# Stick-breaking attention over the prompt: weights formed on VectorE, or the running product applied to differences of values

## The chip, the cores and the metric

One NeuronCore of one Trainium2 chip runs the whole step in one launch. The metric is device time in microseconds (us) of one execution; three executions were timed, and the median is what counts.

## The reference, cut to what matters

One layer of a hybrid encoder trunk: a prompt of 1024 tokens and a sample of 32 tokens with 128 cached positions, model width 1024. A combined projection of the normed input feeds three mixers (an S5 state-space mixer, a gMLP spatial gate, and stick-breaking attention with 8 heads of 64) and three sigmoid gates of 1024 columns each. The gated sum is projected, added, and followed by a SwiGLU. What the change touches is this:

```python
z = einsum("bhtd,bhsd->bhts", q, k) * 64 ** -0.5
causal = k_pos < q_pos
log_1m = where(causal, log_sigmoid(-z), 0)
between = cumsum(log_1m, reverse=True) - log_1m
wts = where(causal, exp(log_sigmoid(z) + between), 0)
o = einsum("bhts,bhsd->bhtd", wts, v)
```

With C(s) the product of sigmoid(-z) over all keys from s to the last, the weight of key s is sigmoid(z(s)) * C(s+1), which is also C(s+1) - C(s).

## The kernel before, in words

All projections are fp32-accurate: every operand is split into a high and a low part (type fp32r), and each product is three matmuls, `mm3` (L142 to L145). A unit of weights, 128 x 1024, is loaded to `raw` (L112), its high part is copied by ScalarE (L116) and its low part subtracted by GpSimd (L117, `split_weights`). The buffers of the weights are a ring of four, two for `raw`.

The program goes through these stages, and on each engine instructions run in the order in which a scheduler has put them at compile time:

- Norm of the input; attention values `v_dense` (L234): a value block is copied from PSUM (L251), written out, then split into high and low halves side by side (L259 on ScalarE, L260 on VectorE) and stored to the DRAM scratch `v_d`. Beside it VectorE computes the tables of the S5 mixer (L396 to L605; L42 to L45 is a complex product, L553 the first transposes on TensorE that need its result, L135 the add that frees a PSUM tile of the sample's values).
- q and k of four pairs of heads (`qk_dense`), the spatial gate, the S5 mixer.
- The prompt's attention (`attention`, L731): 32 units of (pair of heads, block of 256 queries, head). `load_head` (L734) fetches the keys and the split values. `stage_a` (L749) forms z, masks it with a product of `identb` and `maskb`, takes sigmoid(-z) into `om` (L776) and sigmoid(z) into `sg` (L777) on ScalarE, and on VectorE the reversed running product (L779, a scan) and the weights (L780):

```python
v.tensor_tensor_scan(rev, rev, rev, 1.0, op0=OP.mult, op1=OP.bypass)
v.tensor_mul(sg[:, 0:n], sg[:, 0:n], om[:, 1:n + 1])
```

  `stage_b` (L784) transposes the weights by TensorE (L797, tile `p_t`), splits them (L805 ScalarE, L806 VectorE; `wth`, `wtl`, on the diagonal `wd`) and applies them to the values (L813, L814, tile `p_av`); the output of each unit is joined and split again (L826 to L829) and stored to `y_d`. Stage A of a unit is written beside stage B of the unit before.
- Between these steps `fill` (L939) takes steps of other work off a list: the remaining q and k, and `gate_ahead` (L921), which computes gate tiles ahead of their turn, three branches of 24 matmuls each (tile `p_d`, L143 to L145), stored to `sig_d`. `AHEAD = (7, 0)` (L87) says how many of the 8 gate tiles of each half of the tokens are made ahead. These instructions have a lower priority (`LATER`), so that the scheduler alone decides where they go.
- The sample's attention (L872), in front of the last unit. What is left of the list follows.
- The gated merge of half 0 (`gates`, L1005), in which tile 7 is computed and tiles 0 to 6 are read back from `sig_d` (`sgg`), the output projection (L1057), then the merge of half 1 with all its gate tiles computed there, the second norm, and the feed-forward in groups of 256 columns (L1100, L1141).

Of the kernel before, what the change touches and what calls it, by code (L numbers as in the profile page):

```python
# [29 lines left out]
EPS = 1e-6  # L30
# [18 lines left out]
def trunk_kernel(ctx: ExitStack, tc: tile.TileContext,  # L49
# [19 lines left out]
    ring = ctx.enter_context(pool("ring", 4))  # L69
# [9 lines left out]
    q_d = [dram.tile([2, 2, 64, T], F32, name=f"q_d{i}") for i in range(4)]  # L79
    k_d = [dram.tile([2, 2, 64, T], F32, name=f"k_d{i}") for i in range(4)]  # L80
    v_d = [dram.tile([TP, 256], F32, name=f"v_d{i}") for i in range(4)]
# [22 lines left out]
    def split_weights(src, hi=None, lo=None):  # L104
        wh = hi if hi is not None else ring.tile([128, 1024], F32R, name="wh")
        wl = lo if lo is not None else ring.tile([128, 1024], F32R, name="wl")
        raw = ring.tile([128, 1024], F32, name="raw", bufs=2)
# [19 lines left out]
    def tm_sample(ps, xt2, us):  # L127
        # rows 0..31: high parts of the sample, rows 32..63: low parts
# [28 lines left out]
    def rstd_of(wk, ss, rows, more=EPS):  # L157
        # 1 / sqrt(ss + more + EPS), from a first guess in the exponent bits
# [39 lines left out]
    # =====================================================================================  # L198
    # Input projection, mixers
    # =====================================================================================  # L200
    xn = [(half_tile(hx, f"xnh{h}", "hx"), half_tile(hx, f"xnl{h}", "hx")) for h in range(2)]

    with ExitStack() as ph1:
        ps1 = ph1.enter_context(pool("ps1", 2, PSUM))
        qk = ph1.enter_context(pool("qk", 1))
# [6 lines left out]
        # sample attention operands kept on chip  # L212
# [21 lines left out]
        def v_dense(wk):  # L234
            us = v_units
            for b, hc in [(b, hc) for b in range(6) for hc in range(2)] + [(b, hc) for hc in range(2) for b in (8, 6, 7)]:
# [17 lines left out]
                vc = wk.tile([128, 4, 128], F32R, name="vc", bufs=2)  # L254
                v4 = v32.rearrange("p (h d) -> p h d", d=64)
                for e in range(2):
                    o = 64 * e
                    hi = vc[:, e::2, o:o + 64]
# [8 lines left out]
        def qk_dense(wk, hp):  # L267
# [20 lines left out]
            # k first: it goes out beside the products of q  # L288
# [107 lines left out]
        def s5_setup(pl, keep):  # L396
# [175 lines left out]
            # the two groups of a pair side by side: rows (g2, c)  # L572
# [50 lines left out]
        def s5_main(pl, S):  # L623
# [70 lines left out]
            # GLU  # L694
# [36 lines left out]
        def attention(at, qk_tasks):  # L731
            cnt = [0]

            def load_head(hp, h2):  # L734
                kt = at.tile([128, TP], F32R, name="kst", bufs=2)
# [6 lines left out]
            ck = sample_past(at)  # L742
            # the first quarter of these stays zero: keys after all queries
            diags = [[at.tile([128, 512], F32R, name=f"wd{i}{e}") for e in range(2)] for i in range(2)]
            for d in diags:
                for a in d:
                    g.tensor_scalar(a[:, 0:128], ident, 0.0, None, op0=OP.mult)

            def stage_a(hp, tp, h2):  # L749
# [3 lines left out]
                q2 = at.tile([128, 2, 256], F32R, name="q2", bufs=3)  # L753
# [4 lines left out]
                for tt in range(2):  # L758
# [23 lines left out]
                    yield ws, 2 * n / 2400.0 + 0.06  # L782

            def stage_b(hp, tp, h2, ws):  # L784
                vt = heads[hp, h2][1]
                av = ps_tile("av")[:, 0:256]
# [36 lines left out]
                a, b = slice(64 * h2, 64 * h2 + 64), slice(64 - 64 * h2, 128 - 64 * h2)  # L823
                yo = at.tile([128, 2, 256], F32R, name="yo", bufs=1)
                ty = yo[:, 1].bitcast(F32)
                s.activation(ty[a], av[b], AF.Copy)  # L826
                v.tensor_add(ty[a], av[a], ty[a])
                s.activation(yo[a, 0], ty[a], AF.Copy)
                v.tensor_sub(yo[a, 1], ty[a], yo[a, 0].bitcast(F32))  # L829
                o = 256 * (tp % 2)  # L830
                sp.dma_start(y_d[4 + hp][tp // 2].rearrange("l p t -> p l t")[a, :, o:o + 256], yo[a].bitcast(F32))
# [11 lines left out]
            for i, u in enumerate(units):  # L843
# [19 lines left out]
                if i == 30:  # L863
                    sample_attention(at, ck)

# [1 line left out]
        def sample_past(wk):  # L867
            ck = wk.tile([128, 8, 64], F32, name="ck")
# [3 lines left out]
        def sample_attention(wk, ck):  # L872
# [4 lines left out]
            cv = wk.tile([128, 1024], F32, name="cv", tag="kst", bufs=2)  # L877
# [5 lines left out]
            for gr in range(2):  # L883
# [4 lines left out]
                # rows (head, t): keys 128.. are visible before t  # L888
                sg = wk.tile([128, 1024], F32, name="sgs", tag="sg", bufs=4)[:, 0:160]
                om = wk.tile([128, 1025], F32, name="oms", tag="om", bufs=3)[:, 0:161]  # L890
# [22 lines left out]
            yo = wk.tile([128, 2, 256], F32R, name="yos", tag="yo", bufs=1)[:, :, 0:128]  # L913
# [304 lines left out]
```

## Time and profile before

| what | value |
|---|---|
| median of three timed executions | 1812.64 us (1804.2, 1812.64, 1814.32) |
| span of the profiled execution, first to last instruction | 1798.5 us |
| outside the span, against the median | 14.1 us |
| mean granted clock of TensorE, share of full speed | 0.981 |
| TensorE matmul busy | 1692.1 us, 94% of the span |
| VectorE, ScalarE, GpSimd busy | 42%, 31%, 30% |

The profiled execution's own time is not listed beside its span; the timed executions lie 5.7 to 15.8 us above it. The shares are means over stages that differ much: the table of stages in the rows below shows where TensorE is not busy. A granted clock of 1.00 is 2.4 GHz; 0.50 would be 1.2 GHz.

### The profile page before, as it was taken

What the parts mean: (1) busy time and instruction counts of PE and PEld (TensorE: products, weight loads), DVE (VectorE), ACT (ScalarE), POOL (GpSimd) and SP (SyncE); (2) the same over time, 40 slices, a digit from 0 to 9 for tenths busy, and PEclk for the clock granted to TensorE, in tenths of its full rate; (3) what the DMA queues carried; (4) which work ended last, traced back from release to release, by engine and by line L of the source; (5) the groups of instructions that cost most, each with busy time, mean ns of one, the idle gap of its engine ahead of it and who ended that gap; (6) DMA issues with size and microseconds to landing.
All of it is one profiled execution on the core that took longest, in us unless ns stands there. A gap on an engine that the chain in (4) does not pass through costs nothing.

```text
span 1798.5 us, 26081 instructions
## 1 busy us (share of the span) xinstructions
PE 1692.1 (94%) x10421; PEld 1489.7 (83%) x10421; DVE 750.3 (42%) x1498; ACT 564.0 (31%) x1066; POOL 542.7 (30%) x397
## 2 busy tenths in 40 slices
PE   6889998997887899999999899999999999999997
PEld 6879887776565677999999798889889889888885
DVE  7964525259999546112235602121131230221215
ACT  5323232356676422223223422112112111111124
POOL 2211212331112133444443233334233223233344
PEclk9999999999999899999999999999999999999998
DMA  6553252574444187423431111111111111111112
GB/s 206 152 131 92 97 133 73 155 230 144 129 129 113 45 269 250 136 84 93 129 95 60 59 47 48 47 48 48 47 37 50 43 36 48 48 47 48 47 34 87
DMA packets 224617, 171.51 MB, mean 95 GB/s; under 512 B 34608, under 2 KB 202576, under 8 KB 224496
## 3 DMA queue, kind: packets, MB, share of 16 engines
q1 hardware_dynamic: 224496, 169.84, 32.0%
q8 instruction: 82, 1.34, 0.3%
q14 instruction: 39, 0.32, 0.1%
HBM read 131.25 MB, written 37.96 MB: 94 GB/s over the span
## 4 chain that ended last, share of the span: by engine, by line
PE 59%; DVE 4%; ACT 2%; issue 1%; DMA 1%; SPq 0%; POOL 0%; POOLq 0%; DVEq 0%; ACTq 0%
PE p L144 19%; PE p L145 19%; PE p L143 19%; PE p L1160 1%; DVE rs_m L168 1%; DMA y<-y_d 1%; DVE rs_m L169 1%; DVE xb L180 0%; PE ptn L185 0%; DMA raw<-in_w_out_dram 0%; PE p_t L797 0%; DVE sg L780 0%; DVE h L1170 0%; DVE yo L829 0%; ACT junk L1173 0%
## 5 line engine op out<-in xcount | busy, mean ns | idle before, releaser
L117 POOL TENSOR_TENSOR wl<-raw,wh 128x1024 fp32r<-128x1024 f32 x164 | 403.4, 2465 | 713.6 <-ACT wh L116 630.0
L144 PE MATMUL p<-x,wh 128*128 128x272 f32 (+1 forms) x1056 | 342.3, 324 | 0.0
L143 PE MATMUL p<-x,wh 128*128 128x272 f32 (+1 forms) x1056 | 341.5, 323 | 0.0
L145 PE MATMUL p<-x,wl 128*128 128x272 f32 (+1 forms) x1056 | 341.4, 323 | 0.0
L116 ACT ACTIVATE wh<-raw 128x1024 fp32r<-128x1024 f32 x164 | 172.7, 1059 | 475.6 <-PE p L145 190.5
L1116 DVE TENSOR_TENSOR sl<-p,sl 128x272 f32<-128x272 f32 (+1 forms) x66 | 34.6, 525 | 463.8 <-PE p L145 463.8
L143 PEld LDWEIGHTS p<-x,wh 128*128 128x128 f32 x1056 | 198.8, 188 | 16.0
L144 PEld LDWEIGHTS p<-x,wh 128*128 128x128 f32 x1056 | 198.8, 188 | 15.9
L145 PEld LDWEIGHTS p<-x,wl 128*128 128x128 f32 x1056 | 198.5, 188 | 15.2
L143 PE MATMUL p_d<-xnh,wh 128*128 128x512 f32 (+1 forms) x456 | 169.0, 371 | 8.0 <-DVE QS L315 4.3
L144 PE MATMUL p_d<-xnl,wh 128*128 128x512 f32 (+1 forms) x456 | 166.3, 365 | 0.0
L145 PE MATMUL p_d<-xnh,wl 128*128 128x512 f32 (+1 forms) x456 | 166.0, 364 | 0.0
L1119 POOL TENSOR_TENSOR act<-sl,act 128x512 fp32r<-128x512 f32 (+2 forms) x66 | 60.9, 923 | 279.3 <-ACT act L1117 279.3
L1170 DVE TENSOR_TENSOR h<-p,h 128x512 f32<-128x512 f32 x160 | 108.2, 687 | 79.3 <-PE p L145 79.3
L144 PE MATMUL p<-wl,act 128*128 128x512 f32 x352 | 137.2, 390 | 1.2 <-POOL wl L117 1.2
L145 PE MATMUL p<-wh,act 128*128 128x512 f32 x352 | 137.1, 389 | 0.0
L143 PE MATMUL p<-wh,act 128*128 128x512 f32 x352 | 136.9, 389 | 0.0
L145 PE MATMUL p<-xnh,wl 128*128 128x272 f32 (+1 forms) x408 | 120.4, 295 | 0.0
L143 PE MATMUL p<-xnh,wh 128*128 128x272 f32 (+1 forms) x408 | 120.0, 294 | 0.0
L144 PE MATMUL p<-xnl,wh 128*128 128x272 f32 (+1 forms) x408 | 119.9, 294 | 0.0
L143 PEld LDWEIGHTS p_d<-xnh,wh 128*128 128x128 f32 x456 | 90.3, 198 | 18.4 <-DVE QS L315 4.8
L144 PEld LDWEIGHTS p_d<-xnl,wh 128*128 128x128 f32 x456 | 90.2, 198 | 8.5 <-issue 0.2
(384 smaller groups left out, 3273.6 us busy)
## 6 DMA issues: line engine op xcount, KB each, us to landing
raw<-in_w_in_dram SPq DMA_DIRECT2D x66, 512.0 KB, 4.0
raw<-in_w_gate_up_dram SPq DMA_DIRECT2D x44, 512.0 KB, 3.8
raw<-in_w_down_dram SPq DMA_DIRECT2D x22, 512.0 KB, 3.4
q<-q_d SPq DMA_DIRECT2D x64, 128.0 KB, 2.9
raw<-in_w_out_dram SPq DMA_DIRECT2D x16, 512.0 KB, 3.5
sig_d<-sga SPq DMA_DIRECT2D x21, 256.0 KB, 2.8
sgg<-sig_d SPq DMA_DIRECT2D x21, 256.0 KB, 3.4
y<-y_d SPq DMA_DIRECT2D x16, 272.0 KB, 5.5
```

Source lines behind the costliest of these rows:

```text
L116: s.activation(wh, raw, AF.Copy)
L117: g.tensor_sub(wl, raw, wh.bitcast(F32))
L143: pe.matmul(ps, ah, bh, start=start, stop=False)
L144: pe.matmul(ps, ah, bl, start=False, stop=False)
L145: pe.matmul(ps, al, bh, start=False, stop=stop)
L168: v.scalar_tensor_tensor(t, y, mh, y, op0=OP.mult, op1=OP.mult)
L169: v.scalar_tensor_tensor(y, t, 1.5, y, op0=OP.add, op1=OP.mult)
L1116: v.tensor_mul(sl[:, 0:n], pu, sl[:, 0:n])
L1119: g.tensor_sub(act[:, e, T + TS + t0:T + TS + t0 + p], sl[:, 0:p], act[:, e, t0:t0 + p].bitcast(F32))
L1160: pe.matmul(ps, act[:, e, TP:T + TS], u[i][:, cs], start=(j == 0 and i == 0), stop=(j == nu - 1 and i == 1))
L1170: v.tensor_add(hr[:, cs], ps, hr[:, cs])
```

## The change

The weights are no longer formed. The running product C itself (`om`) is transposed and applied to differences of neighbouring values. `v_dense` stores the values unsplit, one row down, behind a row of zeros. `load_head` reads them twice, as `va` (each key's predecessor) and `vb` (the key itself), in rows of one head's 64 columns, with 4 extra blocks whose last key counts as zero, and forms the difference and its split with one VectorE subtraction, one ScalarE copy and another VectorE subtraction. The first quarter of the diagonal tiles is one instead of zero. The two heads of a pair take turns in each block of queries and share one output tile, so that an output step handles 64 x 512 instead of 64 x 256 twice. `AHEAD` goes from (7, 0) to (7, 4): 12 more gate units of half 1, each 48 matmuls of 272 columns, and the credit of the fill list rises (`ratio` 0.7 to 1.0). The ring of weights is one pool up to the end of the attention and another after it. Buffers change: `kst` 2 to 3, `vt` 2 to 3, `q2` 3 to 2, `om` 3 to 4.

```diff
-    AHEAD = (7, 0)
+    AHEAD = (7, 4)
...
 def v_dense(wk):
+            z = wk.tile([1, 128], F32, name="vz")
+            v.memset(z, 0.0)
+            for i in range(4):
+                sp.dma_start(v_d[i][0:1, :], z)
...
-                    s.activation(hi, v4[:, e::2, :], AF.Copy)
-                    v.tensor_sub(vc[:, e::2, 64 - o:128 - o], v4[:, e::2, :], hi.bitcast(F32))
                 for i in range(2):
-                    sp.dma_start(v_d[2 * hc + i][t0:t0 + 128, :],
-                                 vc[:, 2 * i:2 * i + 2].rearrange("p a b -> p (a b)").bitcast(F32))
+                    sp.dma_start(v_d[2 * hc + i][1 + t0:129 + t0, :], v32[:, 128 * i:128 * i + 128])
...
             def load_head(hp, h2):
-                vt = at.tile([128, 8, 128], F32R, name="vt", bufs=2)
-                sp.dma_start(vt.bitcast(F32), v_d[hp].rearrange("(sb s) c -> s sb c", s=128)[:, :, 128 * h2:128 * h2 + 128])
+                va = at.tile([128, 12, 64], F32, name="va", bufs=1)
+                vt = at.tile([128, 12, 2, 64], F32R, name="vt", bufs=3)
+                vb = vt[:, :, 1, :].bitcast(F32)
+                for tl, r0 in ((va, 0), (vb, 1)):
+                    src = v_d[hp][r0:r0 + TP, 64 * h2:64 * h2 + 64].rearrange("(b s) c -> s b c", s=128)
+                    sp.dma_start(tl[:, 0:8], src)
...
+                v.tensor_sub(va, va, vb)
+                s.activation(vt[:, :, 0, :], va, AF.Copy)
+                v.tensor_sub(vt[:, :, 1, :], va, vt[:, :, 0, :].bitcast(F32))
...
-                    sg = at.tile([128, 1024], F32, name="sg", bufs=4)
-                    om = at.tile([128, 1025], F32, name="om", bufs=3)
-                    g.memset(om[:, n:n + 1], 1.0)
+                    om = at.tile([128, 1024], F32, name="om", bufs=4)
...
                         s.activation(om[:, c0:c0 + e], z[:, 0:e], AF.Sigmoid, scale=-0.125)
-                        s.activation(sg[:, c0:c0 + e], z[:, 0:e], AF.Sigmoid, scale=0.125)
                     rev = om[:, 0:n][:, ::-1]
                     v.tensor_tensor_scan(rev, rev, rev, 1.0, op0=OP.mult, op1=OP.bypass)
-                    v.tensor_mul(sg[:, 0:n], sg[:, 0:n], om[:, 1:n + 1])
-                    ws.append(sg)
+                    ws.append(om)
...
-                        lhs = vt[:, 2 * p + 1 - i, :]
+                        b = 8 + p if p == tp and i == 0 else 2 * p + 1 - i
+                        lhs = vt[:, b].rearrange("p l d -> p (l d)")
...
+                if h2:
+                    ty = at.tile([64, 512], F32, name="ty")
+                    yo = at.tile([64, 2, 512], F32R, name="yo")
+                    s.activation(ty, av2[64:128], AF.Copy)
+                    v.tensor_add(ty, av2[0:64], ty)
+                    s.activation(yo[:, 0], ty, AF.Copy)
+                    v.tensor_sub(yo[:, 1], ty, yo[:, 0].bitcast(F32))
...
-            units = [(hp, 3 - tp if 2 * hp + h2 == 7 else tp, h2) for hp in range(4) for h2 in range(2) for tp in range(4)]
-            ratio = 0.7
+            units = [(hp, 3 - tp if hp == 3 else tp, h2) for hp in range(4) for tp in range(4) for h2 in range(2)]
+            ratio = 1.0
```

Where the scheduler puts things, from the compiled programs:

GpSimd from the start of the attention (the last of the four `wd` tiles) to the merge (first CAST, L1053). Each `wl` row is the split of one weight unit, so it shows which units are made ready where; `sgs` and `oms` belong to the sample's attention. Before, its end:

```order
L117 TENSOR_TENSOR wl<-raw,wh 128x1024
L766 MEMSET om 128x1 x5
L117 TENSOR_TENSOR wl<-raw,wh 128x1024
L897 AFFINE_SELECT sgs<-sgs 32x32 x4
L897 AFFINE_SELECT oms<-oms 32x32 x4
L897 AFFINE_SELECT sgs<-sgs 32x32 x4
L897 AFFINE_SELECT oms<-oms 32x32 x4
L117 TENSOR_TENSOR wl<-raw,wh 128x1024 x28
```

In the change, from the last `wd` tile on:

```order
L760 TENSOR_SCALAR wd_3616<-ident 128x128
L118 TENSOR_TENSOR wl<-raw,wh 128x1024 x7
L915 AFFINE_SELECT sgs<-sgs 32x32 x4
L915 AFFINE_SELECT oms<-oms 32x32 x4
L915 AFFINE_SELECT sgs<-sgs 32x32 x4
L915 AFFINE_SELECT oms<-oms 32x32 x4
L118 TENSOR_TENSOR wl<-raw,wh 128x1024 x46
```

Before, 13 units are split between the start of the attention and the sample's part, most of them singly between `om` memsets; now 7. Between the sample's part and the merge's first CAST there are 46 instead of 28, 18 more, though the merge of half 1 has 12 fewer of its own to come. On TensorE the same move counts 271 fill matmuls of 512 columns between the first and the last matmul of the attention before, and 118 now; behind the last one stand 22 before, and now 165 of 512 columns and 576 of 272.

VectorE in the attention, the end of the pair's longest blocks of queries (the scan is printed as SCALAR_TENSOR_TENSOR on `om`). Before:

```order
L806 TENSOR_TENSOR wtl<-p_t,wth 128x512
L780 TENSOR_TENSOR sg<-sg,om 128x896
L829 TENSOR_TENSOR yo<-yo 64x256
L806 TENSOR_TENSOR wtl<-p_t,wth 128x512
L779 SCALAR_TENSOR_TENSOR om<-om 128x1024
L806 TENSOR_TENSOR wd_3678<-p_t,wd_3677 128x384
L780 TENSOR_TENSOR sg<-sg,om 128x1024
```

In the change:

```order
L789 SCALAR_TENSOR_TENSOR om<-om 128x896
L820 TENSOR_TENSOR wtl<-p_t,wth 128x512 x2
L789 SCALAR_TENSOR_TENSOR om<-om 128x1024
L820 TENSOR_TENSOR wd_3616<-p_t,wd_3615 128x384
L750 TENSOR_TENSOR va<-va,vt 128x768
```

The product of `sg` and `om` behind each scan is gone; a subtraction of a head's values, 128 x 768, is new, and its second one stands some nine instructions later.

VectorE beside the attention values, around the second add of the sample's values (L135, in the change L136), which TensorE waits for. Before:

```order
L260 TENSOR_TENSOR vc<-v_1349,vc 128x2x64 x2
L45 TENSOR_TENSOR Ei<-te 128x8x16
L468 TENSOR_TENSOR sm<-Er 128x8
L135 TENSOR_TENSOR v_1376<-p_d,v_1376 32x256
L469 TENSOR_TENSOR sm<-Ei 128x8
```

In the change:

```order
L45 TENSOR_TENSOR Ei<-te 128x8x32
L40 TENSOR_TENSOR te<-Er 128x512
L41 TENSOR_TENSOR te<-Ei 128x512
L136 TENSOR_TENSOR v_1324<-p_d,v_1324 32x256
L42 TENSOR_TENSOR Er<-te 128x8x64
```

The 26 splits of values (`vc`) in front of it are gone, and the add stands 13 table instructions further on. On TensorE the first transposes that need the tables (L553) have moved forward by 34 rows.

## Rows read from the trace of the kernel before

**Rows 1.** Stages: span, length; busy PE, PEld, DVE, ACT, POOL; clock; DMA; GB/s.

```profile
0.00:125.00 125.00, 98.41 (x701) 91.79 (x702) 107.19 (x411) 53.35 (x117) 29.72 (x24) 0.96 0.58 166
...
382.00:606.00 224.00, 186.47 (x1088) 140.45 (x1087) 210.05 (x262) 155.67 (x346) 37.64 (x71) 1.00 0.45 129
...
600.00:620.00 20.00, 16.12 (x85) 12.36 (x84) 9.60 (x21) 6.18 (x16) 6.51 (x17) 0.79 0.21 60
...
606.00:634.00 28.00, 25.89 (x116) 19.89 (x115) 8.47 (x19) 6.11 (x15) 6.36 (x17) 0.72 0.13 37
...
652.00:705.00 53.00, 48.40 (x215) 38.45 (x215) 45.32 (x49) 14.17 (x17) 21.13 (x9) 0.99 0.78 259
705.00:940.00 235.00, 235.00 (x1871) 235.00 (x1871) 49.94 (x82) 62.32 (x94) 99.33 (x52) 0.99 0.38 117
```

**Rows 2.** VectorE's instructions by line in the attention, 382 to 606 us.

```profile
L779 DVE TENSOR_TENSOR_SCAN om<-om 128x256 f32<-128x256 f32 (+7 forms) x63 | 88.9, 1426 | 0.2
L780 DVE TENSOR_TENSOR sg<-sg,om 128x256 f32<-128x256 f32 (+7 forms) x63 | 60.1, 960 | 5.4 <-issue 2.2 <-ACT sg L777 1.2
L806 DVE TENSOR_TENSOR wtl<-p_t,wth 128x512 fp32r<-128x512 f32 x48 | 32.0, 677 | 1.6 <-ACT wth L805 1.3
L806 DVE TENSOR_TENSOR wd<-p_t,wd 128x384 fp32r<-128x384 f32 x31 | 16.9, 546 | 3.4 <-ACT wd L805 3.1
L829 DVE TENSOR_TENSOR yo<-yo 64x256 fp32r<-64x256 f32 x28 | 13.2, 471 | 1.4 <-ACT yo L828 1.0
L827 DVE TENSOR_TENSOR yo<-p_av,yo 64x256 f32<-64x256 f32 x28 | 11.6, 415 | 1.8 <-ACT yo L826 1.3
```

**Rows 3.** What TensorE waited for in the attention: total us, times, longest.

```profile
PE p_t L797 <- DVE wtl L806: 12.5, 11, 2.4
PE p_t L797 <- DVE sg L780: 9.5, 12, 2.5
```

**Rows 4.** VectorE in order of time: start us, duration us.

```profile
428.86 1.21 DVE L780 TENSOR_TENSOR sg<-sg,om 128x1024 f32<-128x1024 f32 x1
...
447.21 0.96 DVE L780 TENSOR_TENSOR sg<-sg,om 128x768 f32<-128x768 f32 x1
...
483.41 2.89 DVE L780 TENSOR_TENSOR sg<-sg,om 128x1024 f32<-128x1024 f32 x1
```

**Rows 5.** GpSimd in order of time, at the last of these.

```profile
482.67 2.55 POOL L117 TENSOR_TENSOR wl<-raw,wh 128x1024 fp32r<-128x1024 f32 x1 [2.55 <-ACT wh L116]
```

**Rows 6.** TensorE in order of time, fill matmuls behind the sample's attention.

```profile
626.50 0.63 PE L144 MATMUL p_d<-xnl,wh 128*128 128x512 f32 x1
626.92 0.63 PE L145 MATMUL p_d<-xnh,wl 128*128 128x512 f32 x1
...
629.30 0.39 PE L144 MATMUL p_d<-xnl,wh 128*128 128x512 f32 x1
629.53 0.39 PE L145 MATMUL p_d<-xnh,wl 128*128 128x512 f32 x1
```

**Rows 7.** What TensorE waited for in the first 360 us.

```profile
PE p_z L553 <- DVE big L42: 5.4, 1, 5.4
PE p_d L143 <- DVE v L135: 5.1, 1, 5.1
```

**Rows 8.** VectorE by line, 20 to 100 us.

```profile
L260 DVE TENSOR_TENSOR vc<-v,vc 128x128 fp32r<-128x128 f32 x32 | 10.2, 357 | 0.1
```

**Rows 9.** DMA by group: KB of one, median us from issue to landing.

```profile
v_d<-vc SPq DMA_DIRECT2D x32, 128.0 KB, 2.4
...
vt<-v_d SPq DMA_DIRECT2D x8, 512.0 KB, 3.8
...
out_dram<-v SPq DMA_DIRECT2D x16, 128.0 KB, 3.8
```

**Rows 10.** What TensorE waited for from 606 to 1100 us.

```profile
PE p L143 <- ACT m L1047: 3.4, 2, 3.1
PE p L145 <- DVE m L1048: 2.4, 3, 1.4
```

More of the change, by code (lines that the diff above doesn't have):

```diff
@@ L68, in trunk_kernel @@
     dram = ctx.enter_context(pool("dram", 1, DRAM))
-    ring = ctx.enter_context(pool("ring", 4))
+    rings = []
     hx = ctx.enter_context(pool("hx", 4))
@@ L80, in trunk_kernel @@
     k_d = [dram.tile([2, 2, 64, T], F32, name=f"k_d{i}") for i in range(4)]
-    v_d = [dram.tile([TP, 256], F32, name=f"v_d{i}") for i in range(4)]
+    v_d = [dram.tile([TP + 1, 128], F32, name=f"v_d{i}") for i in range(4)]
     vs_d = dram.tile([32, 512], F32, name="vs_d")
@@ L104, in split_weights @@
     def split_weights(src, hi=None, lo=None):
-        wh = hi if hi is not None else ring.tile([128, 1024], F32R, name="wh")
-        wl = lo if lo is not None else ring.tile([128, 1024], F32R, name="wl")
-        raw = ring.tile([128, 1024], F32, name="raw", bufs=2)
+        wh = hi if hi is not None else rings[-1].tile([128, 1024], F32R, name="wh")
+        wl = lo if lo is not None else rings[-1].tile([128, 1024], F32R, name="wl")
+        raw = rings[-1].tile([128, 1024], F32, name="raw", bufs=2)
         o = 0
@@ L734, in load_head @@
             def load_head(hp, h2):
-                kt = at.tile([128, TP], F32R, name="kst", bufs=2)
+                kt = at.tile([128, TP], F32R, name="kst", bufs=3)
                 sp.dma_start(kt.bitcast(F32), k_d[hp][h2].rearrange("l d t -> (l d) t")[:, 0:TP])
-                vt = at.tile([128, 8, 128], F32R, name="vt", bufs=2)
-                sp.dma_start(vt.bitcast(F32), v_d[hp].rearrange("(sb s) c -> s sb c", s=128)[:, :, 128 * h2:128 * h2 + 128])
+                va = at.tile([128, 12, 64], F32, name="va", bufs=1)
[4 more added lines that the diff above has]
+                    sp.dma_start(tl[:, 0:8], src)
+                    if r0:
+                        sp.dma_start(tl[0:127, 8:12], src[0:127, 1::2])
+                        sp.dma_start(tl[127:128, 8:12], v_d[hp][0:1, None, 64 * h2:64 * h2 + 64].to_broadcast([1, 4, 64]))
+                    else:
+                        sp.dma_start(tl[:, 8:12], src[:, 1::2])
+                v.tensor_sub(va, va, vb)
+                s.activation(vt[:, :, 0, :], va, AF.Copy)
+                v.tensor_sub(vt[:, :, 1, :], va, vt[:, :, 0, :].bitcast(F32))
                 return kt, vt
             heads = {}
-            ck = sample_past(at)
             diags = [[at.tile([128, 512], F32R, name=f"wd{i}{e}") for e in range(2)] for i in range(2)]
             for d in diags:
-                for a in d:
-                    g.tensor_scalar(a[:, 0:128], ident, 0.0, None, op0=OP.mult)
+                for e, a in enumerate(d):
+                    g.tensor_scalar(a[:, 0:128], ident, 0.0, 1.0 - e, op0=OP.mult, op1=OP.add)
             def stage_a(hp, tp, h2):
@@ L776, in stage_a @@
                         s.activation(om[:, c0:c0 + e], z[:, 0:e], AF.Sigmoid, scale=-0.125)
[L777 removed]
                     rev = om[:, 0:n][:, ::-1]
                     v.tensor_tensor_scan(rev, rev, rev, 1.0, op0=OP.mult, op1=OP.bypass)
[L780 to L781 removed]
+                    ws.append(om)
                     yield ws, 2 * n / 2400.0 + 0.06
+            avs = {}
             def stage_b(hp, tp, h2, ws):
                 vt = heads[hp, h2][1]
[L786 removed]
+                if h2 == 0:
+                    avs[hp, tp] = ps_tile("av")
+                av2 = avs[hp, tp]
+                av = av2[:, 256 * h2:256 * h2 + 256]
                 hl = {}
@@ L822, in stage_b @@
                 apply(tp)
[L823 to L831, printed above, removed]
+                if h2:
[5 more added lines that the diff above has]
+                    v.tensor_sub(yo[:, 1], ty, yo[:, 0].bitcast(F32))
+                    o = 256 * (tp % 2)
+                    for e in range(2):
+                        sp.dma_start(y_d[4 + hp][tp // 2].rearrange("l p t -> p l t")[64 * e:64 * e + 64, :, o:o + 256],
+                                     yo[:, :, 256 * e:256 * e + 256].bitcast(F32))
                 yield 0.44
-            units = [(hp, 3 - tp if 2 * hp + h2 == 7 else tp, h2) for hp in range(4) for h2 in range(2) for tp in range(4)]
-            ratio = 0.7
+            units = [(hp, 3 - tp if hp == 3 else tp, h2) for hp in range(4) for tp in range(4) for h2 in range(2)]
+            ratio = 1.0
             def run_a(u):
@@ L863, in attention, with sample_attention @@
                 if i == 30:
-                    sample_attention(at, ck)
+                    sample_attention(at)
         def sample_past(wk):
-            ck = wk.tile([128, 8, 64], F32, name="ck")
+            ck = wk.tile([128, 8, 64], F32, name="ck", tag="va", bufs=1)
             sp.dma_start(ck, cache_sb_k[0, 0].rearrange("h s d -> s h d"))
             return ck
-        def sample_attention(wk, ck):
+        def sample_attention(wk):
+            ck = sample_past(wk)
             pt = ps_tile("t")
@@ L976, in trunk_kernel @@
             fill(1.0)
+    rings.append(ctx.enter_context(pool("ring", 4)))
     late = ctx.enter_context(pool("late", 1))
```

16 lines of the change are left out of this document (6 added, 10 removed).

## The prediction, made before the changed kernel was run

> **What bounds the kernel now.** I read the stages first. TensorE is busy all 235 us from 705 to 940, and over the whole span it stands idle for 106 us (1798.5 less 1692.1 busy). The change adds and removes no product on TensorE: the same columns are transposed and applied, and the gates of half 1 are computed earlier rather than more often. So the time can only move through TensorE's idle time and its clock, and each part below asks which idle time it touches.
>
> The largest piece is the attention, 382 to 606 us: of 224 us TensorE is busy 186.5 and idle 37.5, while VectorE is busy 210.05, which is 94% [rows 1]. VectorE's groups there say with what: the scan 88.9 us, the weights' product L780 60.1, the splits `wtl` and `wd` 48.9, the outputs 24.8, in all 222.7 with the overlap of neighbouring instructions counted twice [rows 2]. TensorE's waits confirm it: the longest sums are for VectorE's `wtl` and for the product L780 [rows 3]. The fill matmuls come in between; TensorE's busy time there is partly work that could stand elsewhere.
>
> Early in the program TensorE waits twice for VectorE, once for the S5 tables (5.4 us) and once for the add on the sample's values (5.1 us) [rows 7], while VectorE is busy 107 of the first 125 us [rows 1].
>
> **The attention, step by step (VectorE).**
> - The product L780 goes: −60.1 us [rows 2].
> - 28 outputs of 64 x 256 on two lines go, −24.8; 16 of 64 x 512 on two lines come. An instruction on 512 columns with one operand in PSUM is `wtl`, 0.677 us [rows 2], so 32 of them cost +21.7.
> - Eight heads bring two subtractions of 128 x 768 each. L780 at that shape took 0.96 us [rows 4]: 16 x 0.96 = +15.4.
> - GpSimd's weight splits get in VectorE's way: L780 on 128 x 1024 took 1.21 us alone and 2.89 beside a split of 2.55 [rows 4, 5]. The splits that met L780 now meet the scans. Seven splits stand in the changed stretch by the order, so this costs between nothing and 7 x 1.7 = 12; I take the middle, +6.
>
> 222.7 − 60.1 − 24.8 + 21.7 + 15.4 + 6 = 181. With the measured ratio of busy time to the sum, 210.05 / 222.7 = 0.943, VectorE is busy 170.7 us, and at the same share of 94% the stretch takes 182 us instead of 224.
>
> That 42 us is not the gain, because of the fill. The order has 153 fill matmuls of 512 columns fewer inside the stretch (271 to 118), and at 0.233 us each (the spacing at full clock, 0.23 [rows 6]) that is 35.6 us of TensorE's work: 186.5 − 35.6 = 150.8 busy in 182, idle 31 instead of 37.5. **The gain here is about 6 us.** The moved work comes back behind the attention: 165 matmuls of 512 columns (38 us) and 576 of 272. The latter run at 235 / 1871 = 0.126 us in the dense stage [rows 1], 72 us, and leave the merge of half 1, where they cost the same. TensorE works without a gap there, as it did from 705 to 940, so this is neutral.
>
> **The early part.** The 32 splits L260 cost VectorE 10.2 us at 0.357 each [rows 8]. By the order 26 of them stood ahead of the add on the sample's values, 9.3 us, but the add now stands behind 13 more instructions on tables, which I put at 0.37 us each, near L260's, 4.8 us. So the add comes 4.5 us earlier and the wait of 5.1 falls to 0.6. At L553 VectorE arrives 10.2 us earlier and TensorE too, by those 4.5 us and by 34 rows moved forward (98.4 us / 701 instructions = 0.14 in that stage [rows 1], 4.8 us in all), 9.3 together: the wait falls from 5.4 by 10.2 − 9.3 to 4.5. Sum 4.5 + 0.9 = 5.4 us; ends 0 (all of it hidden by new order) and 10.5 (both waits gone).
>
> **The end of half 1's merge.** Four gate tiles that were computed are now read back, in a row. That is the situation of half 0's end: in 652 to 705 VectorE is busy 45.3 of 53 us, TensorE idle 4.6 [rows 1], and two waits for `m` cost 5.8 [rows 10]. Half 1 is 272 wide twice where half 0 has 512, and four tiles instead of seven, so 5.8 x 4/7 = 3.3: I take +3, between 0 and 6.
>
> **At no cost.** ScalarE loses one of two sigmoids and gains eight copies; it is busy 156 of 224 us [rows 1], and VectorE covers it. The memsets of GpSimd went beside VectorE's work; without cover a short one would cost TensorE nothing as nobody waits for GpSimd in the list of waits [rows 3]. The new ring of weights starts behind the attention under the dense block; if that cover failed, one unit's load and split would show, 2.55 us of it the split [rows 5], the rest the load's 3.8 [rows 9]. Twenty-four more stores and twelve more loads of gate tiles go out while the DMA engines are busy 38% [rows 1]. `q2` with two buffers instead of three is loaded one unit ahead, and a unit's 182 / 32 = 5.7 us cover that load; a late one would cost the difference.
>
> **Sum.** −6.3 − 5.4 + 3 = −8.7 us against a span of 1798.5: 1789.8. The median of the timed runs lies 14.1 us above the span, so 1803.9: I forecast **1804 us**. A measurement of this kernel tells about 0.5%, 9 us, from no change, so this is right at that edge.
>
> **The rivals.**
> - *VectorE stops being the bound.* If TensorE, with nothing to wait for, closes up to its need of 151 us plus 12 us for short blocks, where a unit's chain of transpose, split and product stands alone (five waits as long as the longest, 2.4 [rows 3]), the stretch takes 163 and the idle falls by 25 rather than 6. For it: VectorE's load per unit falls by a fifth, and its waits [rows 3] are where the product sat. Against: VectorE still has 171 us. It needs scans undisturbed by splits, and subtractions cheaper than 0.96. 1812.6 − 25 − 5.4 + 3 = 1785. Chance 0.2.
> - *The values come late.* The change loads a head's values twice, in rows of 256 bytes, half as many again as before. 128 KB in rows of 256 bytes took 3.8 us (`out_dram`) where 512-byte rows took 2.4 (`v_d`), and the old 512 KB load 3.8 [rows 9]. So a head takes 3.8 us if nothing is lost and 3.8 x 1.5 x 3.8/2.4 = 9.0 if both count. `va` has one buffer, so the second head's load can start only when the first's subtraction is done; between them stand 12 instructions of VectorE, three `wtl`, three `wd`, an output and four short scans, some 6.2 us by the means [rows 2]. VectorE then stands up to 2.8 us in its queue, with scans behind it that the next transposes need, and the two subtractions, 1.9, come after: 4.7 at each of three changes of pair, 14 us: 1818, no change. Chance 0.17. The Trainium skill, "DMA: Bandwidth & Descriptors", section Specifications, has line rate only from 512 bytes up, with a read-modify-write below; by that rule the upper end, 1818, is the time. That the rows agree for stores, 3.8 against 2.4, is all that this trace shows; no row has a 256-byte load.
> - *The clock falls in the attention (slower).* With TensorE waiting, its granted clock can go from 2.4 to 1.2 GHz: at 600 to 620 us TensorE is busy 16.1 of 20 us and the clock is 0.79, and over 606 to 634 it is 0.72, which costs 28 x 0.28 = 7.8 us [rows 1]; fill matmuls of 512 columns are 0.42 us apart there, then 0.23 [rows 6]. The order takes more than half of the fill out of the attention, and at each change of pair both heads now come to their shortest blocks together, in which TensorE waits for the chain. If what happens at 606 us happens there as well, three more times at 8 us, 24 us are lost: 1804 + 24 = 1828. [...] Against: over the whole attention the clock is 1.00 at 83% busy [rows 1], and 151 of 182 is 83% again. Chance 0.15.
> - That the change does not do what it says is excluded by the order: product and splits are gone.
>
> **How the numbers follow.** The forecast keeps 0.48. Its own bounds are 1790 (both early waits gone, no tail, no collisions, which shortens the stretch by 6) to 1818 (nothing early, tail 6, collisions 6 more). Faster by over 0.5% means below 1803.6: half of the forecast's cases, 0.25, and VectorE off the bound, 0.2: 0.45. Within 0.5% lie the rest of it and the late values: 0.23 + 0.15 = 0.38. Slower by that much: the clock, 0.15, and late values with their full price on top of a tail, 0.02: 0.17. The range reaches from 1782 to 1823: it takes in the forecast, the late values and most of the free VectorE, and leaves out the clock's case.
>
> **What would show it.** VectorE 94% busy in an attention of about 182 us, with TensorE idle some 31 us, confirms the first step; 165 us or less says rival one; a VectorE wait for the `va` DMA at three places rival two; slices with PEclk below 9 inside the attention rival three. Behind the sample's part there should be a block of `p_d` matmuls of 110 us without a gap at full clock. The wait for the sample's add should be below 1 us and the one at L553 between 3 and 5. I am wrong if the attention keeps more idle time than it had, or if the moved work behind it does not run dense.

## The result, and the profile after

The change is slower: the median of 17 runs is 1827.45 us against 1810.45 for 17 runs of the kernel before, the ratio **1.0093, 95% interval 1.0066 to 1.012**. 1804 us was forecast, with 1823 as the upper end and 0.17 for slower by over 0.5%. The profiled execution has a span of 1816.8 us, 18.3 more than before. The times of each of the two kernels lie in two groups some 12 us apart (the profiles of both are from the faster group, and the last section shows a stretch in which profiles differ), so versions are compared by the ratios over all their runs, and profiles stretch by stretch.

The stages after, with the columns of [rows 1]:

```profile
382.00:606.00 224.00, 177.74 (x1039) 137.21 (x1037) 167.84 (x200) 116.59 (x231) 18.96 (x22) 0.93 0.47 124
606.00:634.00 28.00, 28.00 (x118) 22.75 (x119) 1.95 (x4) 5.97 (x8) 8.65 (x4) 0.91 0.71 241
...
652.00:705.00 53.00, 53.00 (x423) 53.00 (x422) 0.00 (x0) 14.55 (x26) 19.26 (x9) 1.00 0.41 124
705.00:940.00 235.00, 228.27 (x1577) 214.78 (x1576) 76.48 (x103) 61.21 (x84) 98.56 (x46) 0.98 0.50 155
...
389.00:590.00 201.00, 162.02 (x963) 126.30 (x963) 162.71 (x187) 112.23 (x223) 14.32 (x5) 0.94 0.51 135
```

The prompt's attention lies between 389 and 590 us now (the sample's follows), and its row stands last. In these 201 us TensorE is idle for 39, at a granted clock of 0.94; before it was 37.5 in 224 at 1.00. VectorE is relieved, 162.7 us busy, but that is 81% and no longer 94: it waits too. Behind it, from 606 to 705, TensorE has no gap: the moved fill runs dense, as was forecast. From 705 to 940, where it had no gap before, it is idle for 6.7 us.

VectorE by line from 382 to 606 us, which answers to [rows 2]:

```profile
L789 DVE TENSOR_TENSOR_SCAN om<-om 128x128 f32<-128x128 f32 (+3 forms) x64 | 91.1, 1435 | 3.0 <-ACT om L787 3.0
L820 DVE TENSOR_TENSOR wtl<-p_t,wth 128x512 fp32r<-128x512 f32 x48 | 31.7, 672 | 7.9 <-ACT wth L819 7.9
L820 DVE TENSOR_TENSOR wd<-p_t,wd 128x384 fp32r<-128x384 f32 x32 | 17.1, 540 | 5.1 <-ACT wd L819 5.1
L844 DVE TENSOR_TENSOR yo<-ty,yo 64x512 fp32r<-64x512 f32 x15 | 10.1, 673 | 0.6 <-ACT yo L843 0.6
L842 DVE TENSOR_TENSOR ty<-p_av,ty 64x512 f32<-64x512 f32 x15 | 10.1, 671 | 2.2 <-ACT ty L841 2.1
L750 DVE TENSOR_TENSOR va<-va,vt 128x768 f32<-128x768 f32 x8 | 7.7, 956 | 38.4 <-DMA vt<-v_d 38.4
L752 DVE TENSOR_TENSOR vt<-va,vt 128x768 fp32r<-128x768 f32 x8 | 7.5, 942 | 1.8 <-ACT vt L751 1.8
```

The product is gone, the two subtractions per head (L750, L752) and the wide outputs are there at the prices that were forecast. New is the idle time in front of L750: VectorE stands 38.4 us for the values, 19.1 of them inside 389 to 590 us. It does so seven times, the longest 19.3 us ahead of the first head.

TensorE's own waits in the attention, which answer to [rows 3]:

```profile
PE p_av L829 <- DVE wtl L820: 16.6, 21, 1.6
PE p_z L781 <- DMA q<-q_d: 12.3, 4, 5.9
PE p_t L811 <- DVE om L789: 6.9, 13, 1.0
PE p_z L781 <- issue: 4.2, 1, 4.2
```

The first product of z waits for the queries four times, 12.3 us, and once 4.2 us for nothing that the profile shows. SP, which issues all these loads, says why. Its queue in order of time at the start of the attention, start and duration of the issues:

```profile
374.14 1.81 SPq L749 DMA_DIRECT2D va<-v_d  x1
376.04 0.82 SPq L744 DMA_DIRECT2D vt<-v_d  x1
376.91 1.37 SPq L746 DMA_DIRECT2D vt<-v_d  x1
378.32 7.05 SPq L747 DMA_DIRECT2D vt<-v_d  x1
385.47 1.30 SPq L768 DMA_DIRECT2D q<-q_d  x2
...
391.50 0.36 SPq L746 DMA_DIRECT2D vt<-v_d  x1
391.91 7.35 SPq L747 DMA_DIRECT2D vt<-v_d  x1
```

A head's values are five loads. L744 loads the 1024 rows, once for `va` and once for `vb` (which is a part of the tile `vt`), and L749 the four extra blocks of `va`. The extra blocks of `vb` come in two loads: L746 has their first 127 rows and L747 the one row of zeros behind them. That last issue, 1 KB, holds SP for 7.05 us for the first head and 7.35 for the second, and only then come the queries (L768). Of the rate of all DMA queues from 370 to 420 us, in 40 slices, this is the row:

```profile
GB/s 416 402 392 197 300 383 296 216 47 18 18 18 19 109 183 317 239 157 162 17 18 18 18 18 104 166 213 316 92 167 3 79 42 199 119 201 181 138 118 219
```

Twice it falls to 18 GB/s and stays there for 5 to 6 us. L746's transfer of 127 x 4 pieces of 256 bytes, 130 KB, is all that is left to move; at 18 GB/s it takes 7.2 us. Of the 16 DMA engines it keeps about one busy (the last two numbers are the DMA share, 0.08, and the GB/s):

```profile
381.50:385.00 3.50, 3.50 (x16) 2.55 (x14) 0.00 (x0) 0.00 (x0) 0.23 (x1) 1.00 0.08 18
```

The second new stop lies behind the dense block. TensorE, and SP at the same time:

```profile
720.87 0.29 PE L146 MATMUL p_d<-xnh,wl 128*128 128x272 f32 x1
724.37 0.80 PE L144 MATMUL p<-xnh,wh 128*128 128x512 f32 x1 [3.21 <-ACT wh L117]
...
726.80 0.79 PE L146 MATMUL p<-xnh,wl 128*128 128x512 f32 x1 [1.21 <-POOL wl L118]
```

```profile
700.54 18.44 SPq L949 DMA_DIRECT2D sig_d<-sga  x7
719.07 1.08 SPq L113 DMA_DIRECT2D raw<-in_w_in_dram  x2
```

The last fill matmul ends at 721, and the merge's first weights are ready at 724.4, their low part at 726.8. Their loads were issued at 719.07, behind seven stores of gate tiles, each of which waits for its tile. The matmuls that follow the low part are 0.43 us apart until 730, at half clock.

### The profile page after: what moved, and what is told of

Same layout as the page of the kernel before. It is cut to its first block, busy times and chain, and to the rows that moved or that the text cites. A ratio compares the mean times of both kernels' runs of the same rounds, so it can differ in the third digit from the quotient of the medians.

```text
span 1816.8 us, 25700 instructions
## 1 busy us (share of the span) xinstructions
PE 1702.1 (94%) x10421; PEld 1502.1 (83%) x10421; DVE 692.2 (38%) x1387; ACT 521.7 (29%) x914; POOL 534.7 (29%) x333
## 4 chain that ended last, share of the span: by engine, by line
PE 62%; DVE 7%; DMA 3%; SPq 3%; issue 2%; ACT 1%; POOL 1%; POOLq 0%; DVEq 0%; ACTq 0%
PE p L146 18%; PE p L145 18%; PE p L144 18%; DMA vt<-v_d 2%; PE p_d L146 2%; PE p_d L144 2%; PE p_d L145 2%; DVE om L789 2%; SPq L747 1%; PE p L1179 1%; DVE rs_m L169 1%; DVE wtl L820 1%; POOL wl L118 1%; DMA raw<-in_w_in_dram 0%; DVE xb L181 0%
## 5 line engine op out<-in xcount | busy, mean ns | idle before, releaser
L144 PE MATMUL p_d<-xnh,wh 128*128 128x272 f32 (+1 forms) x648 | 222.1, 343 | 9.0 <-DVE QS L313 4.4
L146 PE MATMUL p_d<-xnh,wl 128*128 128x272 f32 (+1 forms) x648 | 220.2, 340 | 1.3 <-POOL wl L118 1.3
L145 PE MATMUL p_d<-xnl,wh 128*128 128x272 f32 (+1 forms) x648 | 219.8, 339 | 0.0
L144 PEld LDWEIGHTS p_d<-xnh,wh 128*128 128x128 f32 x648 | 125.9, 194 | 21.0 <-DVE QS L313 4.8
L146 PEld LDWEIGHTS p_d<-xnh,wl 128*128 128x128 f32 x648 | 125.4, 194 | 12.0 <-POOL wl L118 1.7
L145 PEld LDWEIGHTS p_d<-xnl,wh 128*128 128x128 f32 x648 | 125.8, 194 | 10.3 <-issue 0.5
L789 DVE TENSOR_TENSOR_SCAN om<-om 128x128 f32<-128x128 f32 (+3 forms) x64 | 91.1, 1435 | 3.0 <-ACT om L787 3.0
L1061 DVE TENSOR_TENSOR acc<-p,sgg 128x272 f32<-128x272 f32 (+1 forms) x24 | 12.4, 522 | 200.4 <-PE p L146 200.4
```

What stands on the lines that cost most here:

```text
L144: pe.matmul(ps, ah, bh, start=start, stop=False)
L145: pe.matmul(ps, ah, bl, start=False, stop=False)
L146: pe.matmul(ps, al, bh, start=False, stop=stop)
```

## The experiments

Each is an edit of the changed kernel or of another experiment, timed in rounds beside the kernel before; the ratio is to that kernel. A difference of two ratios is uncertain by some 0.0045, or 8 us, if their intervals are taken together, and by 0.006 where a version has few runs (e5 to e7).

**e1_rows112: the 127 rows in two parts.**

```diff
-                        sp.dma_start(tl[0:127, 8:12], src[0:127, 1::2])
+                        for a, e in ((0, 112), (112, 127)):
+                            sp.dma_start(tl[a:e, 8:12], src[a:e, 1::2])
```

> The changed kernel with one edit: the load of the last 127 rows' extra value blocks is split into 112 and 15 rows. Theory A (that load runs on one DMA engine, SP stands behind it for 7 us per head, and what SP issues next, the queries and the next head's values, comes late): the two stops of TensorE at the start of the attention (4.2 and 5.9 us) and those for the queries at the changes of pair (1.4, 3.2, 1.8) go, some 16 us, and the half clock that follows each of them (24 us of it in the attention, a loss of some 10) goes for the most part: 18 to 26 us faster than the changed kernel, ratio to before 0.995 to 1.000, no SP issue above 2 us at the fix-up row. Theory B (the clock falls because the fill has left the attention): the two stops at the start go, the falls of the clock at the changes of pair stay: at most 10 us faster than the changed kernel, ratio 1.004 or more. Theory C (rows of 256 bytes are slow in themselves): the wait of VectorE for the values stays above 5 us per head, no gain.

Measured: 0.9959 (0.9923 to 0.9994), so 0.0134 or 24 us less than the changed kernel: theory A, at the upper part of its range. The issues of the two parts on SP, all 16 of them (duration min, median, max in ns, first and last start in us):

```profile
L747 SPq DMA_DIRECT2D vt<-v_d x16: 496/531/2291, 389.8 to 533.9; - x16
```

The median issue takes 0.53 us, and the row of zeros behind it 0.63 instead of 7.1. Rows of 256 bytes are still what is loaded, and VectorE waits for the values only once, 14.1 us ahead of the first head, so theory C falls. The scheduler put even less fill into this attention (91 matmuls of 512 columns against 118), so theory B falls as well.

**e2_one_ring: one ring of weights.**

```diff
-    rings = []
+    rings = [ctx.enter_context(pool("ring", 4))]
...
-        rings.append(ph1.enter_context(pool("ring1", 4)))
...
-    rings.append(ctx.enter_context(pool("ring", 4)))
```

> The changed kernel with the one ring of weights of the kernel before in place of the two pools. If the first unit of the merge cannot be loaded until the first ring's pool has been left, TensorE's stop of 3.2 + 1.2 us behind the dense block goes, and the 6.8 us at half clock behind it: 7 to 8 us faster than the changed kernel, ratio to before 1.005. If the merge's first weights are late for another reason (SP, the order), no difference.

Measured: 1.0035 (1.0002 to 1.0068), 0.0058 or 10 us less than the changed kernel. TensorE has no wait for weights there any more, and SP's queue in that place shows loads between the stores again (`sig_d` stores are L948 here):

```profile
694.87 0.38 SPq L113 DMA_DIRECT2D raw<-in_w_in_dram  x1
695.35 3.69 SPq L948 DMA_DIRECT2D sig_d<-sga  x2
700.91 0.38 SPq L113 DMA_DIRECT2D raw<-in_w_in_dram  x1
```

Whether the boundary between the two pools held the loads back, or only the order that the scheduler chose with it, this run does not separate.

**e3_both: both edits.**

> Both edits of the two runs above. If the two losses are apart in time and add up: 25 to 34 us faster than the changed kernel, ratio to before 0.990 to 0.996. If the falls of the clock only move to another place, less than the sum of the two.

Measured: **0.9909 (0.9878 to 0.994)**, 1789.56 us: 0.0184 less than the changed kernel, the sum of the two (0.0192). Freed of these two losses the change is faster than the kernel before, by 16 us. The prompt's attention (398 to 580 us) and the sample's behind it, and TensorE's waits in the first:

```profile
398.00:580.00 182.00, 156.97 (x963) 123.34 (x962) 159.40 (x190) 110.10 (x222) 10.70 (x4) 0.98 0.54 145
580.00:597.00 17.00, 13.63 (x61) 9.90 (x59) 3.52 (x11) 3.08 (x8) 6.07 (x17) 0.65 0.13 35
```

```profile
PE p_av L829 <- DVE wtl L820: 10.0, 20, 1.4
PE p_t L811 <- DVE om L789: 9.0, 16, 1.8
```

The stretch is 182 us, VectorE 88% busy in it, TensorE idle for 25, at a clock of 0.98. The queries are waited for once, 0.3 us.

**e4_ahead70: AHEAD = (7, 0) in the changed kernel.**

```diff
-    AHEAD = (7, 4)
+    AHEAD = (7, 0)
```

> The changed kernel with AHEAD = (7, 0) as before, so that the merge of half 1 computes all its gate tiles. If the four tiles read back in a row cost what the profile shows (2.3 us of waits and 3.4 us at half clock at 800 us, less 0 to 2 that the computed ones cost elsewhere): 2 to 4 us faster than the changed kernel, ratio to before 1.007 to 1.008. If the tiles ahead bring something, slower than the changed kernel.

Measured: 1.0078 (1.0048 to 1.0107), which covers the changed kernel's 1.0093: not to be told apart.

**e5_row_first: the row of zeros ahead of the 127 rows** (the two issues change places).

> The changed kernel with the two loads of the fix-up in the other order: the single row of zeros first, the 127 rows behind it. Theory A1 (the 127 rows go one packet after the other on one DMA engine, and whatever SP issues next waits for them): the stop of about 7 us stands then at the load of the queries that follows, the values land as late as before, and the time is that of the changed kernel within 4 us. Theory A2 (it is the single row that holds SP, for instance its repeated source): SP issues on at once, and 10 us or more are gained.

Measured: 1.0135 (1.0089 to 1.018), no gain; the interval covers the changed kernel's 1.0093. The stop has moved to whatever comes next:

```profile
389.05 1.43 SPq L746 DMA_DIRECT2D vt<-v_d  x1
390.53 0.41 SPq L747 DMA_DIRECT2D vt<-v_d  x1
391.04 6.90 SPq L768 DMA_DIRECT2D q<-q_d  x2
```

L747 is now the transfer of 127 rows and issues in 0.41 us, and the two loads of queries behind it (L768) hold SP for 6.9. So it is not the repeated row: the long transfer delays the next one that SP issues. That is A1.

**e6_onchip: e3_both, the extra blocks made on the chip.**

```diff
-                    if r0:
-                        for a, e in ((0, 112), (112, 127)):
-                            sp.dma_start(tl[a:e, 8:12], src[a:e, 1::2])
-                        sp.dma_start(tl[127:128, 8:12], v_d[hp][0:1, None, 64 * h2:64 * h2 + 64].to_broadcast([1, 4, 64]))
-                    else:
-                        sp.dma_start(tl[:, 8:12], src[:, 1::2])
-                v.tensor_sub(va, va, vb)
+                v.tensor_sub(va[:, 0:8], va[:, 0:8], vb[:, 0:8])
+                v.scalar_tensor_tensor(va[:, 8:12], vb[:, 1:8:2], ident[:, 127:128], va[:, 1:8:2], op0=OP.mult, op1=OP.add)
```

> The run with both edits (rows in two parts, one ring), and the four extra blocks made on the chip: two loads per head instead of six, VectorE subtracts 128 x 512 and adds the last key's row with one more instruction of 128 x 256. If the loads still cost something at the changes of pair (issue on SP, rows of 256 bytes): up to 6 us faster than that run, ratio to before 0.988 to 0.991. If they are covered: no difference within 3 us, since VectorE's 0.15 us per head more is nothing.

Measured: **0.9849 (0.9805 to 0.9894)**, 1777.33 us, the fastest version of all. It is a little better than was expected, and its interval overlaps that of e3_both at the edge; the two weren't run side by side. It beats both kernels.

**e7_vsplit: e3_both with the old splits of the values put back in the early part, unused.**

```diff
+                vc = wk.tile([128, 4, 128], F32R, name="vc", bufs=2)
+                v4 = v32.rearrange("p (h d) -> p h d", d=64)
+                for e in range(2):
+                    o = 64 * e
+                    hi = vc[:, e::2, o:o + 64]
+                    s.activation(hi, v4[:, e::2, :], AF.Copy)
+                    v.tensor_sub(vc[:, e::2, 64 - o:128 - o], v4[:, e::2, :], hi.bitcast(F32))
```

> The run with both edits, with the 32 splits of the values put back on ScalarE and VectorE in the early part, their result unused. The forecast's step (VectorE freed by 10 us lets the tables and the add on the sample's values come earlier, 5.4 us): 4 to 6 us slower than the run with both edits. If the chain of the tables sets the pace there, as the trace of the changed kernel shows (the add at 80.2 us and not earlier): within 2 us of it.

Measured: 0.9896 (0.9842 to 0.9951) against 0.9909: no loss. The second add on the sample's values stands at 80.51 us, with the splits ahead of it, where e3_both has it at 81.44 without them:

```profile
80.51 0.41 DVE L136 TENSOR_TENSOR v<-p_d,v 32x256 f32<-32x256 f32 x1
```

But the run moved two things: its scheduler also put the add back ahead of the steps of the tables that stand before it in e3_both. TensorE's waits for this add and for the tables (L551 in the changed kernel) are 11.5 us in all, and 9.7 in e3_both. So the early part may have gained some 2 us by the waits; the times show no gain, and their interval does not rule out 4.

**e8_fill_in: e3_both with the fill in the attention.**

```diff
+        low[0] = 500
         with pool("at", 1) as at:
             attention(at, qk_tasks)
```

> The run with both edits, with the priority of the fill set so that the scheduler puts 295 fill matmuls of 512 columns into the attention (91 there). The forecast's step that moved work costs the same behind the attention: no difference within 4 us. If fill in the attention's gaps takes idle time that is otherwise lost (28 us there) and keeps the clock up (20 us at half clock): 8 to 15 us faster. If fill only delays the chain of transposes and splits: slower.

Measured: 0.9985 (0.9957 to 1.0012), 0.0076 or 14 us more than e3_both. The attention with the sample's, from the first product of z to the last product with the values, here and in e3_both:

```profile
388.60:635.90 247.30, 217.53 (x1217) 171.29 (x1216) 177.16 (x200) 127.00 (x245) 42.50 (x30) 0.94 0.49 134
```

```profile
399.60:596.90 197.30, 168.90 (x1013) 131.83 (x1012) 161.97 (x200) 112.98 (x228) 16.77 (x21) 0.95 0.50 134
```

It is 50 us longer, and the 204 matmuls more are 47.5 us at 0.233 each; TensorE is idle 29.8 us in it, and 28.4 in e3_both. So the fill by itself costs inside what it costs behind, within 3 us. Most of the 14 us lie ahead of the attention, which starts 8.6 us later than in e7_vsplit (380.0) though less work stands ahead of it. TensorE's waits from 320 to 400 us:

```profile
PE p_av L144 <- ACT yh L697: 9.0, 1, 9.0
```

The new priority has taken 33 matmuls on `p_d` out of the stages ahead of the attention (1056 stand there, 1089 in e3_both), and the end of the S5 mixer is waited for, 9.0 us where e7_vsplit waits 1.5. The run was meant to move fill at one place and moved it at two; that its total is slower says nothing on the attention.

**e10_e3_ahead70: e3_both with AHEAD = (7, 0).**

> The run with both edits (rows in two parts, one ring), with AHEAD = (7, 0): the four gate tiles of half 1 are computed in their merge. If the tiles read back in a row cost what their waits show (2.8 us) and moving the rest is neutral: 1 to 4 us faster than the run with both edits. If the block behind the attention needs them (more work between the attention and the merge in which loads and splits catch up): slower by 3 us or more.

Measured: 0.9958 (0.9926 to 0.9991), against 0.9909 (0.9878 to 0.994): 9 us slower by the middle, but the intervals overlap. Inconclusive; a gain by leaving the tiles out is unlikely.

**e11_product_back: e3_both with one VectorE instruction behind each scan.**

```diff
+            one = at.tile([128, 1], F32, name="one")
+            v.memset(one, 1.0)
...
                     v.tensor_tensor_scan(rev, rev, rev, 1.0, op0=OP.mult, op1=OP.bypass)
+                    v.tensor_mul(om[:, 0:n], om[:, 0:n], one.to_broadcast([128, n]))
```

> The run with both edits, with one VectorE instruction put back behind each scan, of the shape and the place of the old weights' product (the running product times one, in place), so that VectorE has 60 us more and the transposes wait for it as before. The scheduler then puts 238 fill matmuls into the attention. If the relief of VectorE is what the change brings: the attention is VectorE's again, and the time goes back to the kernel before or above it, ratio 0.998 to 1.008 (the two subtractions per head, 15 us, are on top). If what the change brings is only that fill has left the attention: the same as the run that put 295 fill matmuls back, 0.9985 within 0.003, with VectorE below 90% in the attention.

Measured: 1.001 (0.9976 to 1.0045), 0.0101 or 18 us more than e3_both. In 400 to 600 us VectorE is busy 192 of 200 us:

```profile
400.00:600.00 200.00, 174.26 (x967) 135.06 (x965) 192.31 (x218) 108.04 (x209) 35.30 (x9) 0.94 0.53 145
```

That is VectorE's attention again, at 96%, where the run with the fill put back had far less (177 of 247). Not all of the 18 us is its price, though. Behind the attention TensorE waits once for the buffer of a gate tile, which e3_both does not:

```profile
PE p_d L144 <- ACT sga L951: 6.9, 1, 6.9
```

The slice from 660 to 680 us has a clock of 0.74 after it. Without that place the relief of VectorE is worth some 8 us by estimate (18 less 6.9 and less some 3 that the low clock takes), which is no more than the noise of the difference; in total time e11 cannot be told from e8.

## Why the prediction was wrong, point by point

**VectorE's sum was near, and the stretch was met by luck, once nothing stands in its way.** 181 us in groups were forecast, and the groups above make 175.3. What is missing is the +6 for GpSimd's splits: a scan takes 1435 ns on average after the change, and took 1426 before. 170.7 us busy in 182, with TensorE idle for 31, was the forecast for the prompt's attention; in e3_both the stretch is 182 us, but VectorE is busy for 159.4 of them, 88% and not the 94% that was carried over. The two misses cancel. TensorE is idle for 25, so the gain in idle time is 12 us where 6 was put, of which the clock of 0.98 takes some 4 back. The first rival's 163 us did not come.

**The values come late: the step that failed.** In the sum this load stood at nothing. It was the second rival, chance 0.17, at 14 us. It happened, and it cost 24 (e1). Its price was a load of 3.8 to 9.0 us per head, by bytes and by a ratio of stores. That ratio was misread too: the stores to `v_d` before have 256 columns of four bytes, so the 2.4 us are for rows of 1024 bytes and not of 512. The rate of a load of 256-byte rows was not the matter. What failed is that the five loads of a head were counted by their bytes together and not one by one with their shapes: the load of 127 rows was taken like one of 128. It runs at 18 GB/s for some 7 us, and the next DMA that SP issues waits with it, the queries among them. The forecast had VectorE alone standing, at three changes of pair; in fact TensorE stands at the beginning as well, 4.2 and 5.9 us, and its matmuls are 0.43 us apart, at half clock, behind each. The Trainium skill, "DMA: Bandwidth & Descriptors", section "Why a DMA increments its semaphore by 16 and not by 1", has it: a transfer is spread over the largest number of engines up to 16 that divides its outer dimension on both sides, and 127 partitions give one. By that rule the 130 KB go through one engine; a DMA share of 0.08, 18 GB/s, and 0.53 us as the median issue once the rows are 112 and 15, agree with it. The forecast weighed another rule of the Trainium skill, line rate only from 512 bytes up (same title, Specifications); as the cause of the loss these runs do not bear it out, since e1 still loads rows of 256 bytes and gains 24 us.

**"At no cost": the ring of weights.** The dense block was named as its cover, and 2.55 + 3.8 us as the price if the cover failed. It failed: 4.4 us of waits and a stretch at half clock behind them in the profile, 10 us by e2. In the profile the loads stand behind the block's stores on SP and are issued 2 us before its end, so the block covers nothing; with one ring they alternate.

**The early part: 5.4 us forecast, some 2 came at most.** After the change:

```profile
PE p_d L144 <- DVE v L136: 6.0, 2, 5.2
...
PE p_z L551 <- DVE big L42: 3.7, 1, 3.7
```

At L551 (L553 before) the wait fell from 5.4 to 3.7, and one of 1.4 for L45, which [rows 7] do not show, is gone; at L551 that is more than was forecast. The wait for the sample's add is 5.2 at its longest, as long as before, because the add itself is later. In all, the waits at the two places went from 11.9 to 9.7 us. The step of the tables that the added instructions follow, and the add, before:

```profile
78.29 0.28 DVE L45 TENSOR_TENSOR Ei<-te 128x128 f32<-128x128 f32 x1
...
78.57 0.41 DVE L135 TENSOR_TENSOR v<-p_d,v 32x256 f32<-32x256 f32 x1
```

After:

```profile
75.36 0.28 DVE L45 TENSOR_TENSOR Ei<-te 128x128 f32<-128x128 f32 x1
...
80.21 0.41 DVE L136 TENSOR_TENSOR v<-p_d,v 32x256 f32<-32x256 f32 x1
```

The 13 instructions take what was put, 4.85 us for 4.8: six of 128 x 256 at 0.42 and two of 128 x 512 at 0.69 make up for the five short ones. The step that failed is the 9.3 us of splits: the same step of the tables starts 2.9 us earlier and not 9.3. The busy time of instructions that are taken away was counted as time by which all that follows moves forward. Where the rest went is not shown.

**The moved work costs the same: right** within 3 us, by e8's attention (50 us for 47.5 of work, 1.4 us of idle time apart).

**The end of half 1's merge: 3 us were forecast, 0.4 came.** The price was taken from the 5.8 us of waits for `m` in [rows 10] as if all were half 0's. Of these, 4.4 are at half 0's end (until 705 us), and 1.4 stood at half 1's end already:

```profile
PE p L145 <- DVE m L1048: 1.4, 1, 1.4
```

After the change half 1's end, 900 to 1100 us, waits 1.8 us:

```profile
PE p L146 <- DVE m L1067: 1.2, 1, 1.2
PE p L144 <- ACT m L1066: 0.6, 1, 0.6
```

Half 0's end waits 2.3 us where it waited 4.4. Whether the tiles ahead gain anything, e4 and e10 leave open.

**The clock.** The third rival's time, 1828, is the time that was measured, by another cause. The clock is low behind each stop of TensorE; with the stops gone and still less fill in the attention, e3_both has 0.98 there. It does fall in the sample's attention, as it did before. That sparse fill lets it fall at the changes of pair is shown by no run.

**The time outside the span.** The sum adds 14.1 us to the span of before; the profiled execution of the change took 1818.52 us for a span of 1816.8, so hardly 2 us lie outside it. In the difference of the two kernels this drops out.

In sum: the change without its two flaws is worth 16 us (e3), where 9 were forecast, and the flaws, put at nothing in the sum, cost 24 and 10. By TensorE's waits, an estimate, some 9 of the 16 are the attention's idle time less its clock, 2 the early part and 3 half 0's end (1.2 us of waits in e3_both); the rest is not traced.

## What to carry to other kernels

Cost every DMA that a change adds by its shape as well as by its bytes, the correction of a single row above all: 127 rows instead of 128 made one load fall to 18 GB/s, and what stood behind it in the issuing queue paid. When buffers are divided among pools, look where the first load of the new pool stands in its queue, and not only at how much work covers it. When a forecast takes instructions away from a busy engine, do not count their busy time as the time by which the next step comes earlier: here 9.3 us were counted and 2.9 came.

## What was not expected of the hardware

One transfer of 127 x 4 pieces of 256 bytes goes at 18 GB/s, with about one of the 16 DMA engines busy, and the next DMA issue on SP's queue is held: 1 KB of zeros for 7.1 us (the median of eight), in e5 two loads of queries for 6.9. Cut into 112 and 15 rows, no issue of it takes more than 2.3.

The granted clock from 290 to 330 us differs between the profiles. The changed kernel, and then e3_both:

```profile
290.00:310.00 20.00, 18.95 (x106) 14.33 (x105) 2.89 (x7) 3.63 (x8) 1.66 (x1) 1.00 0.19 49
310.00:330.00 20.00, 19.88 (x112) 17.14 (x111) 11.00 (x9) 8.62 (x12) 8.95 (x3) 1.00 0.60 138
```

```profile
290.00:310.00 20.00, 19.29 (x71) 14.40 (x70) 2.97 (x6) 1.90 (x4) 2.14 (x1) 0.62 0.19 49
310.00:330.00 20.00, 20.00 (x83) 16.14 (x83) 6.25 (x4) 4.43 (x10) 3.64 (x1) 0.61 0.12 37
```

At 0.62 and 0.61 instead of 1.00 for 40 us, that is 15 us of TensorE's time. The profiles of e1, e3 to e6, e10 and e11 have it; those of before, after, e2, e7 and e8 have not. What sets it off was not found, and as each version has one profile, that the same kernel runs now with it and now without is not shown.
